# Elementwise work of two token mixers moved from GpSimd to VectorE in a two-layer hybrid diffusion block

## The chip, the cores and the metric

The kernel runs on one core of a Trainium2 chip. The metric is the time of one execution on the device in microseconds (us). Three runs of the kernel before took 3043.42, 3047.25 and 3040.82 us, median 3043.42. One more execution was taken under the hardware profiler; all rows of the profile below are of that one.

The engines are named as the profile names them: PE (TensorE, matmuls; PEld its weight loads), DVE (VectorE), ACT (ScalarE), POOL (GpSimd) and SP (SyncE, which here issues most DMAs). Each engine executes its own instructions strictly in the order in which the program gives them, and waits at an instruction until what it needs is there.

## The reference

Two layers over 1024 latent tokens and 256 context tokens of width 1024. In each layer one normalised input goes through one projection, whose columns are shared by three mixers that run side by side; their outputs are joined by one output projection, and a squared-ReLU MLP follows.

```python
h = modulate(rmsnorm(x, g_norm1[l]), sh1, sc1)
pf, mq, mk, mv, mo, mg, cq, ckv, kr = split_proj(h @ w_in[l])
y_f = fourier_mix(pf)                       # real part of a 2-D FFT over (positions, 64 channels)
hf, _ = mlstm_direction(fwd, st_f, False)   # forward and backward mLSTM, 4 heads of 96
hb, _ = mlstm_direction(bwd, st_b, True)
y_m = mlstm_output(hf, hb, mo, g_mlstm[l])  # rmsnorm(hf + hb) * g * sigmoid(mo)
y_a = merge_heads(blocked_attend(qn, qr, (lat_keys, ctx_keys)))   # 4 heads
x = x + ga1 * (jnp.concatenate([y_f, y_m, y_a], axis=-1) @ w_out[l])
x = x + ga2 * sqrelu_mlp(modulate(rmsnorm(x, g_norm2[l]), sh2, sc2), w_up[l], w_down[l])
```

The mLSTM is a recurrence over chunks with a state C per head, which the reference writes as

```python
h = num / jnp.maximum(jnp.abs(den), jnp.exp(-m_t))[..., None]
C_new = decay[..., None, None] * C + jnp.einsum("bhs,bhsd,bhsv->bhdv", wk, kb, vb)
```

where num and den hold the weights within a chunk, exp(dmat − m_t), and the state's part, weighted by w_inter. Everything is in fp32. In layer 0 the context tokens go through the same mixers; in layer 1 only the latent outputs are needed.

## The kernel before

Tokens are cut into ten chunks of 128 (eight latent, two context). Large matmuls run on two rounded halves of each fp32 operand: `split` (L145 to L148) writes the high part with a copy and the low part with a subtraction, and a product then takes three matmuls (L138, L143, L144). Intermediate results of the projection lie in HBM (du, dk, dq, dv for the mixers' inputs; dM and dW for the mLSTM's gate rows; dC for its states; dy for the outputs), and the mixers load them again in tiles.

Attention is the mixers' main work on PE. For each head and block of queries it runs over ten key tiles: three matmuls give the scores s, ACT takes their exponential PT (L1140), and a matmul adds PT times V to v (L1141); below, such a round is called an attention step. The row maxima are found ahead of time, by matmuls into m (L1003) and a reduction on DVE (L1004); a second reduction (L1010) joins them, PE transposes them (L1013), and a split puts them into a row of the queries Q. The queries of the next block are prepared by `q_piece` (rotary part at L989 to L991, then a split).

The other two mixers are written as generators, and `side_work()` pulls one step of them at a time between attention steps: first all of `mlstm`, then `fourier`. That fixes in which neighbourhood their instructions lie. The final order on each engine is set by a scheduler from its own model of the program, and is static: it can move an instruction ahead of others on its engine, but at run time every engine goes through its list in order.

`mlstm` has three parts.

- The recurrence (L825 to L853): 9 steps for each of two directions d, so 18 in a layer. A step loads a chunk's keys kc and values vc (`load_v`, with a memset of a column of ones), transposes the keys on PE (L834), copies them to kt, multiplies vc by a weight per row and head into wv (L839; the tile shares its buffers with Mb, and the profile calls it Mb), multiplies on PE (L842), and updates the state C on DVE (L850, four instructions; the tiles share their buffers with qw and Wb). C goes to dC.
- The output loop (L874 to L927): for each of 10 chunks (layer 1: 8) PE makes the scores sp (L885), and for both directions a step loads Mb and Wb, broadcast from rows of dM and dW; makes tm = mask − Mb (L897), its exponential on ACT (L900), its product with the scores (L901, DVE); qw = qc × Wb (L906), except in a direction's first chunk; and on PE the sums of tm times vc (L912) and qw times the state Cp (L914). DVE then makes the denominators dn (L918 to L920) and hd (L922).
- `tail` (L854 to L872), for the chunk before: hsum = both directions' hd (L856), its square on ACT, a reduction and `rstd_small` (L171 to L187), which is three rounds of L185, L186 and L187 on four columns; two products (L863, L865), three transposes on PE (L868), and the output's store.

`fourier` (L717 to L811) folds the columns of its input uT (the profile calls the tile krw) into sums `up` and differences `um` (L740, L741), folds those again on DVE (L751), and multiplies by tables on PE. It runs for two halves of the channels, in layer 0 for latent and context tokens.

The tiles Mb, tm, qw, Wb, vc and kc have two buffers each; ssb, up, um and uT have one.

Of the kernel before, what the change touches and what calls it, by code (L numbers as in the profile page):

```python
# [9 lines left out]
ALU = mybir.AluOpType  # L10
# [53 lines left out]
def build(tc, A, out, dbg=None):  # L64
# [41 lines left out]
    V, S, G, PE = nc.vector, nc.scalar, nc.gpsimd, nc.tensor  # L106
# [321 lines left out]
    for l in range(2):  # L428
# [83 lines left out]
        for b in range(3):  # L512
            t0, n, w = BLK[b]
            if b < 2 or ctx_all:
                for i in range(2):
# [3 lines left out]
                    o = T(wk, [128, 512], tag="ev")  # L519
# [128 lines left out]
        for n_, ti in enumerate((4, 5, 2, 3, 0, 1)):  # L648
# [18 lines left out]
            wv = cvh[:, ti * 5:ti * 5 + 5]  # L667
# [50 lines left out]
        def fourier(fo):  # L718
# [9 lines left out]
            for i in range(2):  # L728
# [5 lines left out]
                for (o, N, scl) in ((0, NL, 1.0), (NL, NCX, 2.0))[:2 if ctx_all else 1]:  # L734
                    lat = N == NL
                    H = N // 2
                    up = T(f0, [128, 513], tag="up")
                    um = T(f0, [128, 513], tag="um")
                    rev = uT[:, o + H:o + N][:, ::-1]
                    G.tensor_tensor(up[:, 1:H + 1], uT[:, o + 1:o + H + 1], rev, ALU.add)  # L740
                    G.tensor_tensor(um[:, 1:H], uT[:, o + 1:o + H], rev[:, :H - 1], ALU.subtract)  # L741
                    S.copy(up[:, 0:1], uT[:, o:o + 1])
                    S.copy(up[:, H:H + 1], uT[:, o + H:o + H + 1])
                    G.memset(um[:, 0:1], 0.0)
# [68 lines left out]
        def mlstm(mlp_):  # L813
# [12 lines left out]
            for p in range(9):  # L826
                for d in range(2):
                    ci = order[d][p]
                    kc = T(mlp_, [96, 4, 128], tag="kc", bufs=2)
                    nc.sync.dma_start(kc, dkh[:, :, tok(ci)])  # L830
                    vc = load_v(ci)
                    ps = T(psL, [128, 512], tag="l")
                    for h in range(4):
                        PE.transpose(ps[:, h * 96:(h + 1) * 96], kc[:, h, :], ident[:96, :96])  # L834
                    kt = T(mlp_, [128, 512], tag="tm", bufs=2)
                    S.copy(kt[:, :384], ps[:, :384])
                    wcol = wkT[:, 64 * d + ci:64 * d + ci + 31:10]
                    wv = T(mlp_, [128, 4, 128], tag="Mb", bufs=2)
                    G.tensor_tensor(wv[:, :, :97], vc, wcol.unsqueeze(2).to_broadcast([128, 4, 97]), ALU.mult)  # L839
                    pc = T(psL, [128, 512], tag="l")  # L840
                    for h in range(4):
                        PE.matmul(pc[:96, h * 97:(h + 1) * 97], kt[:, h * 96:(h + 1) * 96], wv[:, h, :97], start=True, stop=True)  # L842
                    C = T(mlp_, [96, 4, 128], tag=("qw", "Wb")[d], bufs=2)
                    pv = pc[:96, :388].rearrange("p (h e) -> p h e", h=4)
                    if p == 0:
                        S.copy(C[:, :, :97], pv)
                    else:
                        for h in range(4):
                            dcol = 40 * d + 10 * h + ci
                            V.scalar_tensor_tensor(C[:, h, :97], prev[d][:, h, :97], decb[:, dcol:dcol + 1], pv[:, h], ALU.mult, ALU.add)  # L850
                    prev[d] = C
                    nc.sync.dma_start(dC[d, ci].rearrange("p (h e) -> p h e", h=4), C[:, :, :97])
                    yield  # L853
            def tail(ci, hs, mo):  # L854
                hsum = hs[0]
                G.tensor_tensor(hsum, hs[0], hs[1], ALU.add)  # L856
                S.activation(hs[1], hsum, AF.Square)
                v4 = T(mlp_, [128, 4], tag="v4", bufs=2)
                V.tensor_reduce(v4, hs[1], AX.X, ALU.add)
                V.tensor_scalar(v4, v4, 1.0 / 96, EPS, ALU.mult, ALU.add)  # L860
                y4 = T(mlp_, [128, 4], tag="y4", bufs=2)
                rstd_small(y4, v4, 4, mlp_)
                V.tensor_tensor(hsum, hsum, y4.unsqueeze(2).to_broadcast([128, 4, 96]), ALU.mult)  # L863
                hf = hsum.rearrange("p h e -> p (h e)")
                V.scalar_tensor_tensor(mo, mo, 1.0, hf, ALU.add, ALU.mult)  # L865
                pt = T(psL, [128, 512], tag="l")
                for i in range(3):
                    PE.transpose(pt[:, i * 128:(i + 1) * 128], mo[:, i * 128:(i + 1) * 128], ident)  # L868
                ym = T(mlp_, [128, 3, 128], tag="ym", bufs=2)
                for i in range(3):  # L870
                    S.activation(ym[:, i], pt[:, i * 128:(i + 1) * 128], AF.Copy, scale=gmh[:, 3 * l + i:3 * l + i + 1])
                nc.sync.dma_start(dy[256:640].rearrange("(i p) t -> p i t", p=128)[:, :, tok(ci)], ym)  # L872

            pend = None  # L874
            for ci in range(10 if ctx_all else 8):
# [14 lines left out]
                for d in range(2):  # L890
# [3 lines left out]
                        v_ = src[64 * d:64 * d + 40].rearrange("(h c) t -> h c t", h=4)[:, ci, :]  # L894
                        nc.sync.dma_start(dst, v_.unsqueeze(0).to_broadcast([np_, 4, 128]))
                    tm = T(mlp_, [128, 4, 128], tag="tm", bufs=2)
                    G.tensor_tensor(tm, msk[:, d].unsqueeze(1).to_broadcast([128, 4, 128]), Mb, ALU.subtract)  # L897
                    for h in range(4):
                        col = 64 * d + 10 * h + ci
                        S.activation(tm[:, h], tm[:, h], AF.Exp, bias=aT[:, col:col + 1])  # L900
# [2 lines left out]
                    if not first:  # L903
                        pi = order[d][order[d].index(ci) - 1]
                        qw = T(mlp_, [96, 4, 128], tag="qw", bufs=2)
                        G.tensor_tensor(qw, qc, Wb, ALU.mult)  # L906
                        Cp = T(mlp_, [96, 4, 97], tag="Cp", bufs=2)
                        nc.sync.dma_start(Cp, dC[d, pi].rearrange("p (h e) -> p h e", h=4))
                    po = T(psL, [128, 512], tag="l")
# [792 lines left out]
```

## Time and profile before

| | us |
|---|---|
| runs | 3043.42, 3047.25, 3040.82 |
| median of the runs | 3043.42 |
| the profiled execution, its own time | 3047.78 |
| its span, first to last instruction | 3046.0 |
| mean granted TensorE clock in the span | 0.957 |
| mixers of layer 0 | 362 to 640 |
| recurrence; output loop; Fourier part of layer 0 | 362 to 430; 430 to 570; 570 to 640 |
| mixers of layer 1 | 1950 to 2200 |
| recurrence; output loop; Fourier part of layer 1 | 1950 to 2030; 2030 to 2150; 2150 to 2200 |

The stretches of the mixers were read from the first and last instruction of their lines; they overlap a little, as the scheduler mixes them, and the first loads of layer 1's Fourier part lie in its recurrence. How to read the rows: in a group, the columns are the line, the engine, the operation, what it writes and reads, shapes, the count (x), then busy us and mean ns, then idle time of the engine ahead of the group and who ended it. In a row in order of time the first two numbers are start and duration in us, and brackets hold the idle time ahead and its releaser. In a table of stretches, each engine's busy us (and count) stand in the order of the header line, then the granted clock, the share of the DMA engines and GB/s. A row of waits names the waiting engine, tile and line, the releaser, total us, times, and the longest.

### The profile page before, as it was taken

What the parts mean: (1) busy time and instruction counts of PE and PEld (TensorE: products, weight loads), DVE (VectorE), ACT (ScalarE), POOL (GpSimd) and SP (SyncE); (2) the same over time, 40 slices, a digit from 0 to 9 for tenths busy, and PEclk for the clock granted to TensorE, in tenths of its full rate; (3) what the DMA queues carried; (4) which work ended last, traced back from release to release, by engine and by line L of the source; (5) the groups of instructions that cost most, each with busy time, mean ns of one, the idle gap of its engine ahead of it and who ended that gap; (6) DMA issues with size and microseconds to landing.
All of it is one profiled execution on the core that took longest, in us unless ns stands there. A gap on an engine that the chain in (4) does not pass through costs nothing.

```text
span 3046.0 us, 40618 instructions
## 1 busy us (share of the span) xinstructions
PE 2841.8 (93%) x14320; PEld 2343.2 (77%) x14320; DVE 2112.7 (69%) x4034; ACT 1179.0 (39%) x2283; POOL 667.8 (22%) x653
## 2 busy tenths in 40 slices
PE   7998998998989999999999899898999899989996
PEld 6887875766868888788887788776767688868885
DVE  8769668642399899767787618368632976678887
ACT  3322244443353333333344523244432544434444
POOL 4212234111300000021224233233122000013334
PEclk7999999999989999999999999899999999999998
DMA  6514575223345544732131212365133443353321
GB/s 238 159 53 127 145 181 154 90 69 113 116 159 174 166 168 155 283 118 85 54 97 42 106 43 84 114 163 144 55 112 127 147 147 103 109 197 97 105 90 56
DMA packets 277872, 376.45 MB, mean 124 GB/s; under 512 B 63396, under 2 KB 154468, under 8 KB 276004
## 3 DMA queue, kind: packets, MB, share of 16 engines
q1 hardware_dynamic: 274788, 366.51, 38.5%
q0 software_dynamic: 576, 4.20, 0.4%
q10 hardware_dynamic: 2304, 3.15, 0.3%
q8 instruction: 113, 1.85, 0.3%
q14 instruction: 91, 0.75, 0.1%
HBM read 283.74 MB, written 90.02 MB: 123 GB/s over the span
## 4 chain that ended last, share of the span: by engine, by line
PE 57%; DVE 19%; DMA 10%; issue 6%; POOL 3%; ACT 3%; SPq 0%; DVEq 0%; POOLq 0%; ACTq 0%
PE mm L138 9%; PE mm L143 7%; PE mm L144 7%; PE v L1141 4%; PE mm L135 4%; PE mm L136 4%; PE mm L134 3%; DVE junk L235 3%; DMA wf<-in_w_mt 2%; DVE A L148 2%; DVE ac L677 2%; PE mm L1466 2%; PE mm L140 2%; PE mm L141 2%; DMA gt<-in_w_mt 2%
## 5 line engine op out<-in xcount | busy, mean ns | idle before, releaser
L138 PE MATMUL mm<-A,wr 128*128 128x512 f32 (+1 forms) x840 | 315.2, 378 | 23.5 <-ACT rb L673 9.7
L135 PE MATMUL mm<-A 128*128 128x512 f32 (+1 forms) x654 | 251.6, 390 | 12.0 <-DVE A L148 9.6
L134 PE MATMUL mm<-A 128*128 128x512 f32 (+1 forms) x654 | 238.2, 388 | 5.6 <-ACT A L147 4.5
L136 PE MATMUL mm<-A 128*128 128x512 f32 (+1 forms) x654 | 243.0, 387 | 0.3 <-DVE A L148 0.3
L138 PEld LDWEIGHTS mm<-A,wr 128*128 128x128 f32 x840 | 162.7, 195 | 53.7 <-ACT rb L673 11.4
L143 PE MATMUL mm<-A,wr 128*128 128x512 f32 (+1 forms) x520 | 196.2, 378 | 3.7 <-DVE A L148 1.6
L144 PE MATMUL mm<-A,wr 128*128 128x512 f32 (+1 forms) x520 | 193.7, 373 | 0.0
L1141 PE MATMUL v<-PT,Vt 128*97 128x512 f32 (+1 forms) x336 | 178.1, 616 | 12.9 <-ACT PT L1140 12.6
L138 PE MATMUL mm<-A,c 128*128 128x512 f32 (+1 forms) x520 | 184.4, 355 | 6.2 <-ACT A L147 5.0
L148 POOL TENSOR_TENSOR wr<-wf,wr 128x512 fp32r<-128x512 f32 x88 | 125.2, 1431 | 289.1 <-ACT wr L147 267.3
L143 PE MATMUL mm<-A,c 128*128 128x512 f32 (+1 forms) x520 | 184.8, 355 | 3.0 <-DVE A L148 2.9
L144 PE MATMUL mm<-A,c 128*128 128x512 f32 (+1 forms) x520 | 182.7, 353 | 1.2 <-DVE c L148 1.2
L147 ACT ACTIVATE A<-wr 128x512 fp32r<-128x512 f32 x188 | 114.2, 625 | 147.9 <-PE mm L135 59.2
L147 ACT ACTIVATE A<-A 128x512 fp32r<-128x512 f32 x174 | 107.0, 625 | 160.0 <-PE mm L135 86.5
L148 DVE TENSOR_TENSOR A<-wr,A 128x512 fp32r<-128x512 f32 x146 | 128.8, 894 | 43.3 <-ACT A L147 29.0
L135 PEld LDWEIGHTS mm<-A 128*128 128x128 f32 x654 | 123.9, 190 | 40.7 <-DVE A L148 12.9
L235 DVE SCALAR_TENSOR_TENSOR junk<-wf,t 128x512 bf16<-128x512 f32 x192 | 131.0, 682 | 32.8 <-DMA wf<-in_w_mt 31.1
L1140 ACT ACTIVATE PT<-s 128x512 f32<-128x512 f32 (+1 forms) x168 | 97.3, 583 | 134.1 <-PE s L144 133.7
L134 PEld LDWEIGHTS mm<-A 128*128 128x128 f32 x654 | 123.1, 189 | 31.2 <-ACT A L147 6.9
L136 PEld LDWEIGHTS mm<-A 128*128 128x128 f32 x654 | 123.5, 189 | 24.8 <-DVE A L148 0.7
L138 PE MATMUL mm<-wr,A 128*128 128x256 f32 x464 | 134.3, 290 | 6.6 <-ACT rb L673 4.7
L143 PE MATMUL mm<-wr,A 128*128 128x256 f32 x464 | 133.9, 289 | 0.0
(497 smaller groups left out, 7938.3 us busy)
## 6 DMA issues: line engine op xcount, KB each, us to landing
wf<-in_w_mt SPq DMA_DIRECT2D x96, 256.0 KB
x<-in_w_up SPq DMA_DIRECT2D x40, 512.0 KB
r<-in_w_up SPq DMA_DIRECT2D x38, 512.0 KB
wr<-in_w_dn SPq DMA_DIRECT2D x36, 512.0 KB
gt<-in_w_mt SPq DMA_DIRECT2D x64, 256.0 KB
da<-wf SPq DMA_DIRECT2D x64, 256.0 KB
da<-p SPq DMA_DIRECT2D x64, 256.0 KB
wf<-in_w_in SPq DMA_DIRECT2D x56, 256.0 KB
```

What stands on the lines that cost most here:

```text
L134: PE.matmul(ps, lh, rh, start=first, stop=False, skip_group_check=True)
L135: PE.matmul(ps, lh, rl, start=False, stop=False, skip_group_check=True)
L136: PE.matmul(ps, ll, rh, start=False, stop=last, skip_group_check=True)
L138: PE.matmul(ps, lh, rh, start=first, stop=False)
L140: PE.matmul(ps, ll, rh, start=False, stop=False)
L143: PE.matmul(ps, lh, rl, start=False, stop=False)
L144: PE.matmul(ps, ll, rh, start=False, stop=last)
L147: (hi or S).activation(dst[0], src, AF.Copy) if (hi is None or hi is S) else hi.tensor_copy(dst[0], src)
L148: (lo or G).tensor_tensor(dst[1], src, f32(dst[0]), ALU.subtract)
L235: V.scalar_tensor_tensor(junk, f, 1.0, cb[w], ALU.mult, ALU.mult, accum_out=(ga, modT[l])[kh][:, w, j:j + 1])
L1140: S.activation(PT[:, :nq], ps[:, :nq], AF.Exp, scale=scale)
L1141: PE.matmul(po[:97, :nq], Vt[kt // 2][:, kt % 2, h % 2], PT[:, :nq], start=i == 0, stop=i == len(kts) - 1)
```

## The change

Six elementwise instructions are written for VectorE (`V.`) where they were written for GpSimd (`G.`). Operands, shapes and everything else stay. In a whole run that is 136 instructions: 36 of L839, 18 of L856, 36 of L897, 34 of L906, and 6 each of L740 and L741. GpSimd keeps in these stages the memsets (vc's ones, um's ends) and splits of attention's operands.

```diff
@@ fourier
                     rev = uT[:, o + H:o + N][:, ::-1]
-                    G.tensor_tensor(up[:, 1:H + 1], uT[:, o + 1:o + H + 1], rev, ALU.add)
-                    G.tensor_tensor(um[:, 1:H], uT[:, o + 1:o + H], rev[:, :H - 1], ALU.subtract)
+                    V.tensor_tensor(up[:, 1:H + 1], uT[:, o + 1:o + H + 1], rev, ALU.add)
+                    V.tensor_tensor(um[:, 1:H], uT[:, o + 1:o + H], rev[:, :H - 1], ALU.subtract)
@@ mlstm, recurrence
                     wv = T(mlp_, [128, 4, 128], tag="Mb", bufs=2)
-                    G.tensor_tensor(wv[:, :, :97], vc, wcol.unsqueeze(2).to_broadcast([128, 4, 97]), ALU.mult)
+                    V.tensor_tensor(wv[:, :, :97], vc, wcol.unsqueeze(2).to_broadcast([128, 4, 97]), ALU.mult)
@@ mlstm, tail
                 hsum = hs[0]
-                G.tensor_tensor(hsum, hs[0], hs[1], ALU.add)
+                V.tensor_tensor(hsum, hs[0], hs[1], ALU.add)
@@ mlstm, output loop
                     tm = T(mlp_, [128, 4, 128], tag="tm", bufs=2)
-                    G.tensor_tensor(tm, msk[:, d].unsqueeze(1).to_broadcast([128, 4, 128]), Mb, ALU.subtract)
+                    V.tensor_tensor(tm, msk[:, d].unsqueeze(1).to_broadcast([128, 4, 128]), Mb, ALU.subtract)
...
                         qw = T(mlp_, [96, 4, 128], tag="qw", bufs=2)
-                        G.tensor_tensor(qw, qc, Wb, ALU.mult)
+                        V.tensor_tensor(qw, qc, Wb, ALU.mult)
```

What the change does to the order on an engine is shown at three places, as the difference of the two programs' lists (− stands only in before at this place, + only in after; a name is a tile with a running number; x is a count).

On DVE in layer 0's output loop, inside a tail (y, rs_t, hd and mo are the tail's; tm, qw and dn belong to the output step of a later chunk):

```order
 L187 SCALAR_TENSOR_TENSOR y_861_4466<-rs_t_4470,y_861_4466 128x4
 L863 TENSOR_TENSOR hd_786_4198<-hd_786_4198,y_861_4466 128x384
+L865 SCALAR_TENSOR_TENSOR mo_4153<-mo_4153,hd_786_4198 128x384
+L901 TENSOR_TENSOR tm_4379<-tm_4379,ssb_4363 128x512
+L901 TENSOR_TENSOR tm_4422<-tm_4422,ssb_4363 128x512
+L897 TENSOR_TENSOR tm_4537<-msk_3489,Mb_4533 128x512
 L918 SCALAR_TENSOR_TENSOR dn_4399<-l_4390,flT_1253 128x4
-L865 SCALAR_TENSOR_TENSOR mo_4153<-mo_4153,hd_786_4198 128x384
+L906 TENSOR_TENSOR qw_4544<-qc_4506,Wb_4534 96x512
 L919 TENSOR_TENSOR dn_4399<-l_4390,dn_4399 128x4
```

The moved L897 and L906 now stand among the tail's and the denominators' short instructions, and the tail's last product (L865) ahead of two L901 and one L897.

On DVE at the start of layer 1's recurrence (Mb here is wv of L839; the tiles of L850 called qw and Wb are states; um and fd belong to the Fourier part, Q and mx to attention):

```order
+L839 TENSOR_TENSOR Mb_16856<-vc_16846,wkT_14941 128x4x97
 L991 TENSOR_TENSOR qf_16908<-qf_16908,q_2718_16910 32x512
-L751 TENSOR_TENSOR fd_19155<-um_19145 128x256 x2
+L850 SCALAR_TENSOR_TENSOR qw_16832<-qw_16751,decb_14943,l_16827 96x97 x4
+L741 TENSOR_TENSOR um_19326<-krw_19312 128x511
 L148 TENSOR_TENSOR Q_16900<-qf_16908,Q_16900 96x512
-L850 SCALAR_TENSOR_TENSOR qw_16832<-qw_16751,decb_14943,l_16827 96x97 x4
+L850 SCALAR_TENSOR_TENSOR Wb_16863<-Wb_16804,decb_14943,l_16858 96x97 x4
 L1004 TENSOR_REDUCE mx_16941<-m_16942 128x1
+L839 TENSOR_TENSOR Mb_16887<-vc_16877,wkT_14941 128x4x97
```

Each L839, which needs a load of vc, is now in the list of the state updates and of attention's reductions, and L741, which needs the load of krw, is in front of a split of Q.

On PE in layer 0's output loop, around the transposes of the first tail (L868; the rows L138 to L144 and L1141 are attention steps, m is of the row maxima):

```order
-L868 MATMUL l_4327<-cst_60,mo_4053 128x128 x3
-L885 MATMUL l_4358<-qc_4351,kc_4349 128x128 x4
+L1013 MATMUL m_5054<-cst_60,m_1022_5052 1x128 x4
 L1141 MATMUL v_4688<-PT_4977,Vt_591_3484 97x512
 L138 MATMUL s_5016<-Q_4286,x_586_3479 128x512
 L143 MATMUL s_5016<-Q_4286,x_586_3479 128x512
 L144 MATMUL s_5016<-Q_4286,x_586_3479 128x512
+L1141 MATMUL v_4688<-PT_5020,Vt_592_3485 97x512
+L138 MATMUL s_5045<-Q_4286,x_586_3479 128x512
+L143 MATMUL s_5045<-Q_4286,x_586_3479 128x512
+L144 MATMUL s_5045<-Q_4286,x_586_3479 128x512
+L868 MATMUL l_4327<-cst_60,mo_4053 128x128 x3
```

The transposes now stand behind two L1141 and two rounds of scores that came after them before. Over a layer, ahead of the last tail's transposes stand 48 matmuls of L1141's kind where 43 stood in layer 0, and 137 where 131 stood in layer 1.

## The prediction

> **What bounds the kernel now.** I read the share of each engine first, then the stretches in which the moved lines run, engine by engine, then PE's waits in them.
> ```profile
> PE 2841.8 (93%) x14320; PEld 2343.2 (77%) x14320; DVE 2112.7 (69%) x4034; ACT 1179.0 (39%) x2283; POOL 667.8 (22%) x653
> ```
> Over the whole run PE is the bound. The moved lines run only where the mixers do, 362 to 640 and 1950 to 2200 us, so the question is what PE lacks there. The stretches are layer 0's recurrence and output loop, then layer 1's:
> ```profile
> core 0: us, PE busy (x) PEld busy (x) DVE busy (x) ACT busy (x) POOL busy (x), PEclk, DMA share, GB/s
> 362.00:430.00 68.00, 61.69 (x414) 49.37 (x412) 41.03 (x115) 26.18 (x55) 20.53 (x45) 0.95 0.79 179
> 430.00:570.00 140.00, 116.27 (x637) 87.75 (x636) 113.92 (x277) 65.98 (x171) 58.55 (x55) 0.91 0.54 144
> 1950.00:2030.00 80.00, 67.42 (x435) 54.94 (x434) 47.06 (x117) 28.48 (x58) 26.67 (x52) 0.89 0.71 172
> 2030.00:2150.00 120.00, 109.84 (x583) 83.06 (x582) 95.16 (x230) 58.24 (x145) 47.69 (x45) 0.91 0.50 133
> ```
> PE is idle 6.3 + 23.7 + 12.6 + 10.2 = **52.8 us** in these 408 us, and its clock is below full: no gain can be larger than that idle time and what of the clock comes back with it. In the output loops DVE is 81% and 79% full, so it has little room for more work, on its face. The next rows are why its fullness is not what it seems: layer 0's output loop, DVE and POOL in order of time.
> ```profile
> 454.75 1.31 POOL L897 TENSOR_TENSOR tm<-msk,Mb 128x512 f32<-128x512 f32 x1 [0.88 <-ACT PT L1140]
> ...
> 454.94 1.13 DVE L185 TENSOR_TENSOR rs_t<-y 128x4 f32<-128x4 f32 x1
> ...
> 456.06 1.28 POOL L906 TENSOR_TENSOR qw<-qc,Wb 96x512 f32<-96x512 f32 x1
> ...
> 456.11 1.25 DVE L186 TENSOR_TENSOR rs_t<-rs_t,rs_h 128x4 f32<-128x4 f32 x1
> 457.39 0.16 DVE L187 SCALAR_TENSOR_TENSOR y<-rs_t,y 128x4 f32<-128x4 f32 x1
> ...
> 457.59 0.16 DVE L185 TENSOR_TENSOR rs_t<-y 128x4 f32<-128x4 f32 x1
> ```
> A DVE instruction on four columns takes 1.13 and 1.25 us, and ends when the GpSimd instruction beside it ends; the same line takes 0.16 us 1.4 us after. So a two-operand instruction of DVE waits, within its duration, for GpSimd's to finish. The busy time of DVE in these stages holds GpSimd's time a second time.
>
> **The change part by part.** All six lines become DVE instructions. What they cost on GpSimd, over the run:
> ```profile
> L897 POOL TENSOR_TENSOR tm<-msk,Mb 128x512 f32<-128x512 f32 x36 | 46.8, 1299 | 117.8 <-PE l L912 83.6 <-DVE qf L991 10.8 <-PE m L144 9.1
> L906 POOL TENSOR_TENSOR qw<-qc,Wb 96x512 f32<-96x512 f32 x34 | 45.5, 1337 | 8.7 <-DMA Wb<-dW 4.4 <-DVE q L990 3.7 <-PE l L914 0.5
> L839 POOL TENSOR_TENSOR Mb<-vc,wkT 128x388 f32<-128x388 f32 x36 | 31.3, 873 | 65.8 <-PE l L842 37.0 <-DMA vc<-dv 24.1 <-PE m L1003 4.8
> L856 POOL TENSOR_TENSOR hd<-hd,hd 128x384 f32<-128x384 f32 x18 | 18.2, 1013 | 55.0 <-DVE hd L922 55.0
> L740 POOL TENSOR_TENSOR up<-krw 128x512 f32<-128x512 f32 (+1 forms) x6 | 6.0, 997 | 36.9 <-PE l L769 36.7
> L741 POOL TENSOR_TENSOR um<-krw 128x511 f32<-128x511 f32 (+1 forms) x6 | 6.0, 996 | 22.9 <-PE l L763 15.6 <-ACT fd L753 4.7 <-DMA krw<-du 2.6
> ```
> That is 153.8 us. On DVE the nearest rows are two-operand instructions of the same shapes (minimum, median and maximum in ns):
> ```profile
> L901 DVE TENSOR_TENSOR tm<-tm,ssb x36: 673/685/1452, 433.1 to 2147.2; 128x512 f32<-128x512 f32 x36
> L865 DVE SCALAR_TENSOR_TENSOR mo<-mo,hd x18: 542/558/1523, 460.9 to 2163.2; 128x384 f32<-128x384 f32 x18
> L186 DVE TENSOR_TENSOR rs_t<-rs_t,rs_h x111: 139/161/2433, 73.1 to 3038.0; 128x4 f32<-128x4 f32 x90, 128x2 f32<-128x2 f32 x21
> L991 DVE TENSOR_TENSOR qf<-qf,q x16: 682/683/2864, 368.1 to 2226.3; 32x512 f32<-32x512 f32 x16
> ```
> **Added to DVE:** 70 instructions of L897 and L906 at 0.685 = 48.0 us, 54 of L839 and L856 at 0.558 = 30.1 us, and 12 of L740 and L741, of which eight are of 512 elements and four of 128, at most 0.685 each = under 8; I take 6.5. Sum 84.6 us. The Trainium skill, "GPSIMD Engine Reference", section 3.1 on elementwise work, puts GpSimd at 1.96 times DVE for such an instruction; by that page the estimate would be 78.5 us, and the rows' 1299 against 685 (1.90) agree.
>
> **Taken from DVE:** the waits inside its instructions. Layer 0's output loop, then layer 1's, at count, sum and mean:
> ```profile
> L186 DVE TENSOR_TENSOR rs_t<-rs_t,rs_h 128x4 f32<-128x4 f32 x24 | 12.0, 498 | 0.6
> L187 DVE SCALAR_TENSOR_TENSOR y<-rs_t,y 128x4 f32<-128x4 f32 x24 | 11.4, 476 | 0.4
> L185 DVE TENSOR_TENSOR rs_t<-y 128x4 f32<-128x4 f32 x24 | 8.7, 364 | 0.5
> L863 DVE TENSOR_TENSOR hd<-hd,y 128x384 f32<-128x384 f32 x8 | 7.5, 940 | 0.4
> L865 DVE SCALAR_TENSOR_TENSOR mo<-mo,hd 128x384 f32<-128x384 f32 x8 | 6.1, 758 | 0.1
> L991 DVE TENSOR_TENSOR qf<-qf,q 32x512 f32<-32x512 f32 x3 | 3.9, 1305 | 0.1
> ```
> ```profile
> L185 DVE TENSOR_TENSOR rs_t<-y 128x4 f32<-128x4 f32 x20 | 8.3, 417 | 0.4
> L186 DVE TENSOR_TENSOR rs_t<-rs_t,rs_h 128x4 f32<-128x4 f32 x20 | 7.4, 371 | 0.4
> L187 DVE SCALAR_TENSOR_TENSOR y<-rs_t,y 128x4 f32<-128x4 f32 x20 | 7.4, 369 | 0.4
> L865 DVE SCALAR_TENSOR_TENSOR mo<-mo,hd 128x384 f32<-128x384 f32 x6 | 5.2, 863 | 0.1
> ```
> With 0.161 for the small, 0.558 for the 384-wide and 0.683 for L991, layer 0 gets back 8.1 + 7.6 + 4.9 + 3.1 + 1.6 + 1.9 = 27.2 us, layer 1 5.1 + 4.2 + 4.2 + 1.8 = 15.3. Added in the same stretches: layer 0 38 instructions at 0.685 and 9 at 0.558 = 31.0; layer 1 32 and 7 = 25.8. So DVE goes from 113.9 to **117.7 of 140** and from 95.2 to **105.7 of 120**: about as full as before, with GpSimd's 106 us of these stretches off the board. In the recurrences 18 instructions add 10 us each to 41 of 68 and 47 of 80: room enough, but for order (below).
>
> **What of it is on PE's path.** PE's waits that hang on GpSimd or on DVE's stretched chain, layer 0 and then layer 1 (total, times, longest):
> ```profile
> PE l L868 <- DVE dn L918: 10.6, 5, 2.8
> ...
> PE m L1013 <- DVE m L1010: 2.9, 1, 2.9
> PE m L1003 <- DVE mx L1004: 2.3, 2, 2.1
> ```
> ```profile
> PE l L842 <- POOL Mb L839: 9.6, 5, 5.5
> PE l L868 <- DVE dn L919: 6.2, 3, 3.8
> PE l L914 <- POOL qw L906: 2.5, 1, 2.5
> ```
> L868 are the transposes that end a tail, the chain of some fifteen short DVE instructions of which the stretched L185 to L187 (three rounds of each) are the middle. Of these 34.1 us I leave 5.5 in place: the longest L839 wait also needs its load of vc, which lands just ahead of it. 28.6 remain. From below they can all stay, since DVE is as full as before (that they grow is the second rival); from above they can all go. I take **half, 14.3**: a tail's instructions no longer pay 1.2 us each, but share their queue with 0.685 us ones. The third order piece above points the same way: two more rounds of attention's scores and L1141 fill PE ahead of the transposes. In the two output loops and layer 1's recurrence the clock's shortfall is 0.09 × 140 + 0.09 × 120 + 0.11 × 80 = 32 us-equivalents; if it follows the idle time, of which 14.3 of 46.5 go, that is 10; I take half, **5**.
>
> **What it costs.** GpSimd waited for loads with nothing of weight behind it; DVE's queue has. The rows above give vc 24.1, Wb 4.4 and krw 2.6 us; Mb is
> ```profile
> POOL tm L897 <- DMA Mb<-dM: 7.1, 1, 7.1
> ```
> In all 38.2 us. Most were waits of an engine that ran ahead, and DVE arrives later. In layer 1's recurrence L839 now stands ahead of L850 (the state that releases PSUM) and L1004 (softmax scores for PE's L1013), so a late vc holds both: **3 us** of the 24.1, between 0 and 24.1. There too um stands ahead of the split of Q, so a late krw delays PE's attention: **2 us**, between 0 and 2.6. In layer 0 and layer 1 the first L897 stands ahead of L850; PE was idle around it before, so 0, up to 7.1. Wb costs 0, up to 4.4: DVE reaches it behind L897, whose load was issued first. L856 opens the tail, and is part of the half taken for L868. L740 and L741 release the Fourier part's folds (L751), and in its stretch of layer 0 PE lacks 1.2 us of 70:
> ```profile
> 570.00:640.00 70.00, 68.80 (x375) 50.26 (x373) 36.97 (x104) 28.25 (x70) 5.55 (x10) 1.00 0.19 62
> ```
> So they gain nothing there, and cannot cost much either, with DVE half full. GpSimd keeps the memsets of these stages and its splits, which now start no later than before; I count nothing for them.
>
> **Sum:** −14.3 − 5 + 3 + 2 = −14.3 us. The profiled execution took 3047.8 us (span 3046.0 and 1.8 around it), so 3033.5; it is 4.4 above the median of 3043.4, so 3029.1, which I give as 3030. A change under 0.2% (6.1 us) can't be told from none here.
>
> **The rivals.** *Even exchange, about 3043.* DVE is as full after as before, and the tail still waits its turn. For it: 117.7 of 140 against 113.9. Against: the POOL waits of PE (12.1 us) end sooner whatever DVE does, since 0.685 replaces 1.3. The Trainium skill, "Perfetto Trace Analysis", section on optimizing Scalar/DVE operations, says that because the two engines share an SBUF read port, moving work between them may not help; the stretched rows above show the sharing, but in them GpSimd's instruction takes twice as long as DVE's would, which that sentence leaves out. Its outcome would be this rival's time.
>
> *Head of the line, slower, about 3055.* DVE takes its queue in order. Where a load of vc, Mb, Wb or krw lands after DVE gets there, everything behind it stands: L1004, L850, the splits of Q. It decides the sign from the point where DVE arrives at such a line ahead of its load by more, summed over a layer's 18 recurrence steps, than the 7 us (half of 14.3) that a layer gains; GpSimd's 38.2 us of such waits are its ceiling, and a third to a half of it, 12 to 19 us, less a small gain of 4, gives 3051 to 3058. For it: DMA is 79% and 71% busy in the recurrences. Against: 24.1 of the 38.2, those for vc, come from instructions that GpSimd reached with nothing else to do, while DVE in the recurrences has 41 of 68 and 47 of 80 us of older work in front of them, which uses up part of each wait.
>
> *The whole of it, about 3012.* All 28.6 go, and the clock pays 5: 33.6 less a little cost, 3012. For it: in PE's new order 48 attention steps (one L1141 each in that list) lie ahead of layer 0's last tail where 43 did, and 137 where 131 did in layer 1, so that PE has more to do while a tail runs. Against: DVE's fullness, and that a tail is a chain, whose links wait for what stands between them in the queue.
>
> That the change doesn't do what it says is out: all 136 instructions stand in DVE's order and none in GpSimd's.
>
> **How the numbers follow.** Forecast (3018 to 3037) 0.40, even exchange (3037 to 3049) 0.25, head of the line 0.18, the whole 0.17. Faster: the forecast and the whole, 0.57; same 0.25; slower 0.18. Low 3010 takes in the whole; high 3056 most of the slower rival.
>
> **What would show it.** Right: L185 to L187 near 0.16 us throughout, PE's waits at L868 halved, DVE near 118 and 106 in the same stages, both stages shorter by 5 to 10 us. Even exchange: L868's waits unchanged with L185 short. Head of the line: DVE idle before L839, L897 or L906 on a DMA, and PE's waits for L1010 or L148 grown. The prediction is wrong at its root if L897 on DVE takes over 1 us, or if L185 stays near 0.4 without GpSimd beside it.

## The result, and the profile after

The changed kernel took 3016.85 us (median of four runs, 3013.96 to 3020.10) where the kernel before took 3042.12 (four runs, 3038.17 to 3047.25): a ratio of **0.9915**, 95% interval 0.9899 to 0.9932, so 25.3 us faster. A second comparison on another occasion gave 0.9909 (0.9896 to 0.9921). The forecast was 3030 in a range of 3010 to 3056, that is 13.4 us faster than the 3043.4 known then: the direction and the range held, but the gain was nearly twice the forecast one. The profiled execution after took 3019.14 us with a span of 3017.3, 28.6 us less than the profiled one before.

Where the time went is seen from stretches with fixed ends: from a layer's first transposed key (L834) to its last attention matmul (L1141), in which each kernel does the same work. Before, then after, layer 0 and layer 1:

```profile
core 0: us, PE busy (x) PEld busy (x) DVE busy (x) ACT busy (x) POOL busy (x), PEclk, DMA share, GB/s
365.80:745.60 379.80, 337.66 (x1766) 247.48 (x1767) 227.63 (x559) 157.48 (x362) 100.54 (x117) 0.95 0.46 122
1960.20:2276.50 316.30, 290.58 (x1497) 215.75 (x1498) 200.63 (x468) 134.84 (x294) 90.02 (x102) 0.93 0.47 127
```
```profile
363.90:722.90 359.00, 330.41 (x1767) 244.53 (x1767) 232.24 (x627) 156.53 (x361) 21.88 (x44) 0.96 0.48 129
1935.70:2247.90 312.20, 290.29 (x1498) 216.70 (x1498) 210.21 (x530) 135.33 (x294) 20.74 (x40) 0.93 0.48 128
```

Layer 0 became 20.8 us shorter and layer 1 4.1. Length less PE's busy time is PE's idle time: 42.1 and 25.7 us before, 28.6 and 21.9 after, so 13.5 and 3.8 us of idle time went. PE's matmuls are the same in the trace but for one record in each layer; they took 7.3 us less in layer 0 (a better clock, 0.96 for 0.95) and 0.3 less in layer 1. DVE, which took some 79 us of GpSimd's work in layer 0, is busy only 4.6 us more there. A second profiled execution of the changed kernel (e6) has 352.9 and 311.7 for the two layers, so in layer 0 differences of less than about 6 us between single profiles are not read below; in layer 1 the two profiles agree to 0.5 us.

DVE's groups in the two output loops, in the windows of the prediction (layer 0's, then layer 1's):

```profile
L897 DVE TENSOR_TENSOR tm<-msk,Mb 128x512 f32<-128x512 f32 x19 | 13.0, 686 | 3.7 <-PE l L912 3.4 <-DMA Mb<-dM 0.2
L906 DVE TENSOR_TENSOR qw<-qc,Wb 96x512 f32<-96x512 f32 x18 | 12.2, 679 | 3.9 <-DMA Wb<-dW 3.9
L185 DVE TENSOR_TENSOR rs_t<-y 128x4 f32<-128x4 f32 x28 | 4.4, 157 | 0.5
L186 DVE TENSOR_TENSOR rs_t<-rs_t,rs_h 128x4 f32<-128x4 f32 x27 | 4.2, 157 | 0.5
L187 DVE SCALAR_TENSOR_TENSOR y<-rs_t,y 128x4 f32<-128x4 f32 x27 | 4.2, 156 | 0.5
```
```profile
L186 DVE TENSOR_TENSOR rs_t<-rs_t,rs_h 128x4 f32<-128x4 f32 x24 | 3.8, 160 | 0.5
```

The small instructions have their 0.16 us everywhere, where their means were 0.36 to 0.50 us before, and tm and qw take 0.686 and 0.679 instead of 1.3. PE's waits in layer 0's mixers and in layer 1's, the lines that answer to those of before:

```profile
PE m L1003 <- DVE mx L1004: 0.4, 1, 0.4
...
PE l L868 <- DVE dn L920: 0.2, 1, 0.2
```
```profile
PE l L842 <- DVE Mb L839: 7.2, 2, 5.2
PE m L1003 <- DVE mx L1004: 3.8, 4, 1.6
PE m L1013 <- DVE m L1010: 3.5, 3, 1.9
...
PE l L868 <- DVE hd L922: 0.4, 1, 0.4
```

The waits at the tails' transposes went almost altogether: 10.6 to 0.2 and 6.2 to 0.4 us. In layer 1 the wait at L1003 is new (0.3 us before, over the whole layer); that at L1013 is not, as the layer had 3.1 us of it before, late in its stretch.

### The profile page after: what moved, and what is told of

Its sections match the earlier page's. It is cut to its first block, busy times and chain, and to the rows that moved or that the text cites. A ratio compares the mean times of both kernels' runs of the same rounds, so it can differ in the third digit from the quotient of the medians.

```text
span 3017.3 us, 40556 instructions
## 1 busy us (share of the span) xinstructions
PE 2827.9 (94%) x14320; PEld 2334.7 (77%) x14320; DVE 2128.6 (71%) x4170; ACT 1178.6 (39%) x2283; POOL 517.3 (17%) x517
## 4 chain that ended last, share of the span: by engine, by line
PE 59%; DVE 18%; DMA 10%; issue 6%; POOL 2%; ACT 2%; SPq 0%; DVEq 0%; POOLq 0%; ACTq 0%
PE mm L138 9%; PE mm L143 7%; PE mm L144 7%; PE v L1141 4%; PE mm L135 4%; PE mm L136 4%; PE mm L134 4%; DVE junk L235 3%; DVE A L148 2%; DVE ac L677 2%; PE mm L1466 2%; PE mm L140 2%; PE mm L141 2%; DMA wf<-in_w_mt 2%; PE t L1466 2%
## 5 line engine op out<-in xcount | busy, mean ns | idle before, releaser
L138 PE MATMUL mm<-A,wr 128*128 128x512 f32 (+1 forms) x840 | 312.9, 375 | 24.6 <-ACT rb L673 12.3
L138 PEld LDWEIGHTS mm<-A,wr 128*128 128x128 f32 x840 | 161.2, 193 | 54.0 <-ACT rb L673 14.0
L143 PE MATMUL mm<-A,wr 128*128 128x512 f32 (+1 forms) x520 | 193.0, 372 | 6.2 <-DVE A L148 4.2
L144 PE MATMUL mm<-A,wr 128*128 128x512 f32 (+1 forms) x520 | 191.6, 369 | 0.0
L1141 PE MATMUL v<-PT,Vt 128*97 128x512 f32 (+1 forms) x336 | 172.8, 599 | 16.6 <-ACT PT L1140 16.1
L138 PE MATMUL mm<-A,c 128*128 128x512 f32 (+1 forms) x520 | 184.0, 355 | 4.5 <-ACT A L147 3.4
L144 PE MATMUL mm<-A,c 128*128 128x512 f32 (+1 forms) x520 | 182.5, 353 | 1.3 <-DVE c L148 1.3
L148 POOL TENSOR_TENSOR wr<-wf,wr 128x512 fp32r<-128x512 f32 x88 | 123.7, 1413 | 292.1 <-ACT wr L147 230.3
L148 DVE TENSOR_TENSOR A<-wr,A 128x512 fp32r<-128x512 f32 x146 | 128.7, 893 | 43.4 <-ACT A L147 29.0
L138 PE MATMUL mm<-wr,A 128*128 128x256 f32 x464 | 133.4, 288 | 6.6 <-ACT rb L673 4.7
```

The source lines that it names most:

```text
L138: PE.matmul(ps, lh, rh, start=first, stop=False)
L143: PE.matmul(ps, lh, rl, start=False, stop=False)
L144: PE.matmul(ps, ll, rh, start=False, stop=last)
L148: (lo or G).tensor_tensor(dst[1], src, f32(dst[0]), ALU.subtract)
L1141: PE.matmul(po[:97, :nq], Vt[kt // 2][:, kt % 2, h % 2], PT[:, :nq], start=i == 0, stop=i == len(kts) - 1)
```

## The experiments

Four theories were set against each other. **A**: the shared port; GpSimd's instructions stretch DVE's, and that lateness reaches PE (in a narrow form at the transposes L868, in a wide form through how full DVE is). **B**: own durations; each moved line is shorter on PE's path by its own 0.6 us. **C**: the scheduler's new order alone. **D**, formed after e4: the stretch costs because the order was planned without it. (No run looks into the scheduler's model; that it leaves the stretch out is what D assumes.)

All ratios are to the kernel before, run beside the experiment on the same chip; the numbers of attention steps are counted in PE's list, as in the order pieces above. Those of layer 1, above and in the expectations, are counted from the program's start and hold the 88 steps of layer 0: 131 and 137 are 43 and 49 of layer 1's own 80. Below they are given within the layer. The expectations name the experiments' theories by these letters.

**e1: tm and qw alone,** on the kernel before, as are e2, e5, e8, e9, e10 and e12.
```diff
-                    G.tensor_tensor(tm, msk[:, d].unsqueeze(1).to_broadcast([128, 4, 128]), Mb, ALU.subtract)
+                    V.tensor_tensor(tm, msk[:, d].unsqueeze(1).to_broadcast([128, 4, 128]), Mb, ALU.subtract)
...
-                        G.tensor_tensor(qw, qc, Wb, ALU.mult)
+                        V.tensor_tensor(qw, qc, Wb, ALU.mult)
```


> Only L897 and L906 (tm, qw) go to VectorE; L839, L856, L740 and L741 stay on GpSimd. Theory A (shared port): the gain comes from the tail's short DVE instructions no longer being stretched by a GpSimd instruction beside them, and tm and qw are what runs beside the tails: 18 to 23 us faster than before (about 3020 to 3024), L186 in layer 0's output loop near 0.2 us, PE's waits at L868 below 3 us in each layer. Theory B (own durations): each moved instruction saves its own 0.6 us on PE's path, so the gain goes with the moved GpSimd time, 92.3 of 153.8 us: about 15 us faster, with L842's waits of layer 1 unchanged. Theory C (order alone): PE's list has L868 behind nearly the same attention steps as in the changed kernel (48 and 138), so all of the gain, 25 us.

Measured 0.9906 (0.9886 to 0.9925), 28 us faster: all of the gain, with 60% of the moved GpSimd time. Theory B, which priced by each line's own time, expected 15, and theory A 18 to 23; the 25 of theory C are nearest.

**e2: wv of the recurrence alone.**
```diff
-                    G.tensor_tensor(wv[:, :, :97], vc, wcol.unsqueeze(2).to_broadcast([128, 4, 97]), ALU.mult)
+                    V.tensor_tensor(wv[:, :, :97], vc, wcol.unsqueeze(2).to_broadcast([128, 4, 97]), ALU.mult)
```


> Only L839 (wv of the recurrence) goes to VectorE. Theory A: the tails keep their GpSimd neighbours, so 0 to 4 us faster, out of L842's waits in layer 1 alone (9.6 us before). Theory B: 31.3 of 153.8 us of GpSimd time, so about 5 us. Theory C: in layer 1 L868 stands as late as in the changed kernel (136 attention steps ahead of the last tail against 137), in layer 0 45 against 48: 8 us or more.

Measured 1.0017 (1.0002 to 1.0032): no gain, if anything a loss. Theory C falls in its plain form, as L868 stands nearly as late in layer 1's list as in the changed kernel (48 steps against 49), and layer 1's mixers took 316.5 us, as before (316.3).

**e4: the changed kernel with GpSimd loaded again.**
```diff
-            pend = None
+            pend = None; dum = T(mlp_, [128, 4, 128], tag="dum")
...
                     V.tensor_tensor(tm, msk[:, d].unsqueeze(1).to_broadcast([128, 4, 128]), Mb, ALU.subtract)
+                    G.tensor_tensor(dum, msk[:, d].unsqueeze(1).to_broadcast([128, 4, 128]), Mb, ALU.subtract)
...
                         V.tensor_tensor(qw, qc, Wb, ALU.mult)
+                        G.tensor_tensor(dum[:96], qc, Wb, ALU.mult)
```


> The changed kernel, and beside each L897 and L906 of VectorE the same instruction once more on GpSimd, into a tile that nothing reads. PE's list stands nearly as in the changed kernel. Theory A: the stretch of L185 to L187 returns (means of 0.35 to 0.5 us instead of 0.16 in layer 0's output loop), PE waits at L868 again by over 8 us in layer 0, and 12 to 25 us of the 25 gained are lost: 3029 to 3042. Also the moved instructions themselves get stretched. Theory B and theory C: nothing waits for the added instructions and the order is that of the changed kernel: 3014 to 3021.

Measured 1.0019 (1.0007 to 1.0031): the whole gain is lost to instructions whose result nobody reads. Its layers, and DVE's groups in layer 0's output loop:

```profile
359.20:731.80 372.60, 336.20 (x1766) 248.76 (x1767) 254.55 (x627) 156.94 (x361) 75.39 (x82) 0.94 0.46 124
1940.00:2267.30 327.30, 299.05 (x1498) 221.55 (x1498) 225.87 (x531) 135.25 (x294) 65.30 (x72) 0.91 0.45 123
```
```profile
L897 DVE TENSOR_TENSOR tm<-msk,Mb 128x512 f32<-128x512 f32 x20 | 16.3, 816 | 8.6 <-PE l L912 4.7 <-DMA Mb<-dM 3.8
L906 DVE TENSOR_TENSOR qw<-qc,Wb 96x512 f32<-96x512 f32 x18 | 14.7, 816 | 2.1 <-DMA Wb<-dW 2.1
L922 DVE TENSOR_TENSOR hd<-l,dn 128x384 f32<-128x384 f32 x20 | 10.9, 551 | 0.2
L185 DVE TENSOR_TENSOR rs_t<-y 128x4 f32<-128x4 f32 x30 | 8.1, 271 | 0.5
L186 DVE TENSOR_TENSOR rs_t<-rs_t,rs_h 128x4 f32<-128x4 f32 x30 | 6.0, 198 | 0.5
```

DVE does the same 627 instructions of layer 0 as in the changed kernel, and is busy 254.6 us instead of 232.2: the stretch is GpSimd's doing. It falls on two-operand instructions in SBUF, tm and qw too (0.816 for 0.686 and 0.679), and not on all of DVE: L922, whose wide operand is in PSUM, has 0.551 us here and 0.552 in the changed kernel. But the tail's small instructions are stretched less than expected (0.20 to 0.27 us), and PE's waits at L868 stayed below 3 us in layer 0: the loss does not sit at the transposes. One thing is mixed in: PE waited 3.0 us at L912 for GpSimd's added instructions, and the one result of GpSimd that L912 uses is the memset of vc, which stands behind them. That is 3.0 of the 7.8 us by which PE's idle time in layer 0 grew (28.6 to 36.4), so e4 does not show the price of the stretch by itself.

**e5: the port as before, the transposes later.**
The second half of tail, from its transposes on, becomes a function of its own, which is called one chunk later:
```diff
+            def tail2(ci, mo):
                 pt = T(psL, [128, 512], tag="l")
...
-                        tail(*pend)
+                        tail(*pend); pend2 = (pend2 and tail2(*pend2), (pend[0], pend[2]))[1]
...
-                mo = T(mlp_, [128, 384], tag="mo", bufs=2)
+                mo = T(mlp_, [128, 384], tag="mo", bufs=3)
```


> The kernel before, all six lines on GpSimd, but the transposes that end a tail (L868) and what follows them are written one chunk later, with a third buffer for mo. The port stays as contended as before. Theory A in its narrow form (PE's waits at L868 are where the stretch costs): these waits go (16.8 us over both layers), and with the clock 12 to 20 us are gained: 3022 to 3030. Theory A in a wide form (DVE's fullness sets the pace of the whole output loop) and theory B: PE finds other waits instead, below 5 us gained: 3037 to 3045. Theory C predicts a gain only where L868 stands later among the attention steps than before, which here is so in layer 1 (135 against 131) and not in layer 0 (42 against 43): about 4 us.

Measured 1.0014 (0.9999 to 1.0029). PE's waits at L868 fell from 10.6 to 7.0 us in layer 0 and from 6.2 to 1.5 in layer 1, and nothing was gained: at L885 PE waited 3.4 and 4.5 us instead of 1.2 and 0.7, and the last tail's transposes stand no later in layer 0's list (42 steps). This speaks against the narrow form of theory A, by which L868 is where the lateness costs; but half of the 16.8 us was still there, so it is not a clean test.

**e6: the changed kernel again.**

> The changed kernel once more, so that the next three stand beside it on the same chip: 0.9915 of before, within 0.9899 to 0.9932.

Measured 0.9909 (0.9896 to 0.9921).

**e7: the same DVE load, on DVE's own account.**
The two added lines of e4, on the other engine:
```diff
-                    G.tensor_tensor(dum, msk[:, d].unsqueeze(1).to_broadcast([128, 4, 128]), Mb, ALU.subtract)
+                    V.tensor_tensor(dum, msk[:, d].unsqueeze(1).to_broadcast([128, 4, 128]), Mb, ALU.subtract)
...
-                        G.tensor_tensor(dum[:96], qc, Wb, ALU.mult)
+                        V.tensor_tensor(dum[:96], qc, Wb, ALU.mult)
```


> The changed kernel with each L897 and L906 done twice on VectorE, the second time into a tile that nothing reads: some 26 us more of DVE work in layer 0's output loop and 22 in layer 1's, which is what the added GpSimd instructions cost DVE before (27.9 and 16), but on DVE's own account, known to the scheduler, and without a port held by another engine. Theory A, wide form (how full DVE is sets the pace, however it comes to be full): all or nearly all of the gain is lost, 0.997 to 1.004 of before. Theory D (what costs is that the stretch falls on instructions whose place was planned without it): the scheduler puts L868 behind 64 attention steps in layer 0 instead of 48, PE is fed, and at least half of the gain stays, 0.991 to 0.996.

Measured 0.9990 (0.9980 to 1.0000). By the total theory A had it, but the layers tell two things apart:

```profile
360.70:717.40 356.70, 331.09 (x1762) 245.72 (x1762) 254.51 (x664) 156.33 (x360) 20.41 (x43) 0.95 0.47 129
1929.20:2261.10 331.90, 299.24 (x1496) 221.81 (x1497) 230.18 (x563) 135.89 (x294) 20.70 (x40) 0.91 0.45 121
```

In layer 0 DVE is as busy as in e4 (254.5 and 254.6 us), and the layer takes 356.7 us instead of 372.6, as short as in the changed kernel. There, DVE work that the order was planned with costs nothing that can be told, and as much of it made by GpSimd's added instructions costs 16 us, with the wait for the memset in it and with another list (64 steps in e7, 53 in e4). In layer 1 both cost about the same (331.9 and 327.3 against 312.2): there the list put hardly more attention ahead of the last tail (52 steps against 49), and why it did not is open.

**e8: hsum alone.**
```diff
-                G.tensor_tensor(hsum, hs[0], hs[1], ALU.add)
+                V.tensor_tensor(hsum, hs[0], hs[1], ALU.add)
```


> Only L856, the sum that opens a tail, goes to VectorE. Theory A: 18 instructions of 1.0 us go from the port, of 92 + 18 us beside the output loops, and DVE gets 10 us more: within 0.2% of before, 0.998 to 1.001. The rival (the tail's chain sets PE's waits, link by link): each tail is 0.45 us shorter by L856 itself, 18 tails, 8 us: 0.996 to 0.998.

Measured 0.9976 (0.9963 to 0.9989): 7 us, as the rival had it. Here the order changed too (46 attention steps ahead of the last tail of layer 0 instead of 43), so the run does not show which of the two it was.

**e9: tm, qw and hsum, without the recurrence's and the Fourier part's lines.** The edit is that of e1 and e8 together.

> L897, L906 and L856 on VectorE, L839, L740 and L741 left on GpSimd. If the lines of the recurrence and of the Fourier part only fill DVE's queue (L839 alone gave 1.0017), this is 0.1 to 0.3% faster than the changed kernel: 0.988 to 0.991. If they pay for themselves where the others are moved too: 0.991 to 0.994.

Measured 0.9908 (0.9896 to 0.9921), against 0.9909 of the changed kernel beside it. So in the whole time L839, L740 and L741 bring nothing and cost nothing that can be told, where the others are moved. The profiles of layer 1 say otherwise: it took 302.8 us in e1 and 304.1 in e9, which leave these lines on GpSimd, and 312.2 and 311.7 in the two of the changed kernel (308.0 in e13). Outside the two stretches e9 took 2348.1 us and e6 2342.0, which makes the totals equal; why is open.

**e10: the kernel before, with one pacing number changed.**
```diff
-RM = (0.5, 0.8)
+RM = (0.9, 0.8)
```


> The kernel before with one number changed: the share of attention's steps over which layer 0's mLSTM is spread, 0.9 instead of 0.5. GpSimd and the port stay as they were. In PE's list of layer 0 the last tail's transposes then stand behind 47 attention steps instead of 43 (48 in the changed kernel), in layer 1 behind 136 instead of 131. Theory D (in layer 0 the stretch costs because the order was planned without it, and PE has other work to put there): layer 0's mixers 8 to 15 us shorter, 0.995 to 0.997 of before in all. Theory A alone (DVE as full, port as contended): 0.999 to 1.002. Theory C (order alone explains the change): 0.991.

Measured **0.9939** (0.9925 to 0.9954), about 19 us faster: more than theory D expected (0.995 to 0.997) and less than theory C (0.991). GpSimd still does all six lines:

```profile
361.80:720.00 358.20, 330.49 (x1766) 245.15 (x1767) 220.87 (x559) 156.23 (x362) 101.10 (x117) 0.96 0.47 129
1928.30:2243.10 314.80, 288.72 (x1496) 212.67 (x1497) 195.33 (x468) 135.07 (x294) 91.05 (x102) 0.93 0.47 128
```

Layer 0 is as short as in the changed kernel (358.2 against 359.0), with GpSimd at 101.1 us as before; layer 1 is as long as before (314.8 against 316.3), though its list has moved to 48 steps. PE's waits at L868 in layer 0 are 3.2 us. The stretch is not quite that of before, however: over layer 0, before and then e10,

```profile
L186 DVE TENSOR_TENSOR rs_t<-rs_t,rs_h 128x4 f32<-128x4 f32 x30 | 12.9, 430 | 0.8
L187 DVE SCALAR_TENSOR_TENSOR y<-rs_t,y 128x4 f32<-128x4 f32 x30 | 12.4, 412 | 0.5
L185 DVE TENSOR_TENSOR rs_t<-y 128x4 f32<-128x4 f32 x30 | 9.7, 323 | 0.7
```
```profile
L187 DVE SCALAR_TENSOR_TENSOR y<-rs_t,y 128x4 f32<-128x4 f32 x30 | 9.5, 317 | 0.6
L186 DVE TENSOR_TENSOR rs_t<-rs_t,rs_h 128x4 f32<-128x4 f32 x30 | 9.1, 303 | 0.7
L185 DVE TENSOR_TENSOR rs_t<-y 128x4 f32<-128x4 f32 x30 | 7.9, 264 | 0.7
```

These three lines took 35.0 us before and 26.5 in e10, where in the changed kernel they take 14.1, so some two fifths of their stretch went with the new list and the rest stayed. DVE's busy time in layer 0 fell by 6.8 us for the same 559 instructions.

**e11 and e12: L922 to ACT,** in the changed kernel and in the kernel before.
```diff
-                    V.tensor_tensor(hd, pv[:, :, 0:96], dn.unsqueeze(2).to_broadcast([128, 4, 96]), ALU.mult)
+                    for h in range(4): S.activation(hd[:, h], pv[:, h, 0:96], AF.Copy, scale=dn[:, h:h + 1])
```


> The changed kernel with L922 (hd from PSUM times 1/dn, 0.55 us on DVE, 36 of them) done by ACT in four pieces: 20 us less DVE work over both layers (about 11 and 9), 20 to 35 us more on ACT, which was half full in the output loops. Theory A (in layer 1 DVE's fullness sets the pace): layer 1's mixers 4 to 9 us shorter than in the changed kernel, layer 0's 0 to 4: 0.987 to 0.990 of before. If DVE's work is no longer what sets the pace once GpSimd is gone: as the changed kernel, 0.990 to 0.993; if ACT's exponentials (L900, L1140) wait behind it, slower than that.

> The kernel before, GpSimd's six lines in place, with L922 on ACT. DVE is relieved of the same 20 us, with the port as contended as before. Theory A: fullness counts however it is made, so 20 of the 41 us (of the stretch) that the change took away come off here too: 0.994 to 0.997. Theory D and the narrow form (the stretch itself, inside the tail's chain): 0.998 to 1.001.

Measured 0.9898 (0.9881 to 0.9914) for e11, not to be told from the changed kernel, and 1.0026 (1.0011 to 1.0041) for e12. In e12 DVE was busy 214.9 us in layer 0's mixers instead of 227.6, and they took 381.6 us instead of 379.8. A less busy DVE alone gains nothing, though ACT was 16.4 us busier for it (173.9 for 157.5), an addition that in e11 (17.3 us) left layer 0 as it was. In layer 1 too, e12 and e11 took 315.5 and 311.2 us, where the kernels without this edit took 316.3 and 312.2. So the wide form of theory A has no support in these two runs.

**e13: the changed kernel, paced slower.** The edit is `RM = (0.82, 0.8)`.

> The changed kernel with layer 0's mLSTM spread over 0.82 of attention's steps. In PE's list of layer 0 the last tail's transposes stand behind 53 attention steps instead of 48. Theory D: PE's waits of layer 0 that are left (26 us of idle time, of which under 3 us at L868, L912 and L914) are not of this kind, so 0 to 3 us: 0.989 to 0.992 of before. If PE's list still lacks filler: 0.986 to 0.989.

Measured 0.9890 (0.9873 to 0.9907), the lowest of all, but its interval meets that of the changed kernel.

Layer 0 in all these kernels, in the order of the attention steps that stand ahead of its last tail's transposes (length and DVE busy time in us, from the profiles):

| kernel | steps | length | DVE busy |
|---|---|---|---|
| e5 | 42 | 375.0 | 226.8 |
| before | 43 | 379.8 | 227.6 |
| e12 | 44 | 381.6 | 214.9 |
| e2 | 45 | 382.5 | 230.3 |
| e8 | 46 | 368.7 | 230.7 |
| e10 | 47 | 358.2 | 220.9 |
| changed (two profiles) | 48 | 359.0, 352.9 | 232.2, 232.2 |
| e1; e9 | 48 | 357.1; 353.1 | 220.2; 224.3 |
| e11 | 52 | 358.3 | 224.4 |
| e13 | 53 | 351.5 | 233.4 |
| e4 (GpSimd loaded besides) | 53 | 372.6 | 254.6 |
| e7 | 64 | 356.7 | 254.5 |

Length does not go with DVE's busy time; with the steps it does: 375 us and more up to 45 steps, 359.0 and less from 47 on, except in e4, where GpSimd's load is added. The number of steps is only one mark of a whole order. A reading that fits all rows is theory D's, that PE is fed in layer 0 when the list puts enough attention ahead of mLSTM steps at the pace that these really have; the runs don't prove it. For layer 1 the steps tell nothing: 48 in e10 with 314.8 us, 49 in e9 with 304.1 and in the changed kernel with 312.2.

## Why the prediction was right, point by point

**The stretch** of DVE's small instructions by GpSimd was read rightly: 0.16 us throughout after, and back again in e4. **DVE's fullness** was forecast at 117.7 of 140 and 105.7 of 120 us; in the same windows it is

```profile
430.00:570.00 140.00, 130.57 (x752) 98.74 (x751) 120.39 (x362) 71.61 (x183) 1.38 (x9) 0.98 0.55 149
2030.00:2150.00 120.00, 115.44 (x616) 88.71 (x617) 101.80 (x298) 58.92 (x140) 1.09 (x6) 0.94 0.50 130
```

120.4 and 101.8, though the second window holds a later part of layer 1 than before. The Trainium skill, "Perfetto Trace Analysis", in its section on optimizing Scalar/DVE operations, doubts that moving work between these two engines helps because they share a port; in layer 0 here DVE took some 79 us of GpSimd's work for 4.6 us of its own busy time, and the kernel was 25.3 us faster.

**The terms of the sum.** The profiled pair differs by 28.6 us: 24.9 in the two stretches and 3.7 outside them. PE's idle time holds the path's gain and the costs together: forecast −14.3 + 5 = −9.3 us, measured −17.3 (13.5 + 3.8). The clock term was −5; PE's busy time fell by 7.6 (7.3 + 0.3). So the sum was short by 8.0 and 2.6 us in the stretches. The mis-sized step is "**half**": half of 28.6 us of waits was held back because DVE would be as full as before. Of these waits about 26 us went, those at L868 almost whole (16.8 to 0.6 us); other waits came in their place, so that the idle time fell by 17.3. In layer 0, e7 and e12 speak against fullness as a brake: there a DVE load that the list is planned with costs nothing that can be told, and relief alone gains nothing. The costs of 5 us (vc 3, krw 2) are not settled: the whole time of e9 beside e6 shows none (0.9908 against 0.9909), the profiles of layer 1 differ by 8 to 9 us between e9 or e1 and the changed kernel.

**The place.** "Both stages shorter by 5 to 10 us" was wrong: layer 0 gained 20.8 us and layer 1 4.1. In layer 1 the wait left in place (L842, 5.5 us) did stay, at 5.2, and a new wait of 3.8 us for the row maxima came (L1003). It is not in e1 and e9, where L839, L740 and L741 stay on GpSimd.

**The reason.** The prediction named the stretch as the cause, and the larger order in PE's list only as support for its "whole of it" rival. e10 turns this about for layer 0: a new list, with all of GpSimd's work and most of the stretch in place, makes the layer as short as the change does, and brings 0.9939 where the change brings 0.9915. e4 points the other way: with a list that has even more steps ahead, and GpSimd loaded again, the gain is gone, though part of that loss is the wait for the memset. Both fit if what counts is the match of list and pace; that is argued, not shown. How much of the 21 us in layer 0 comes from the new list and how much from the missing stretch is not settled, since no kernel here has the changed kernel's list with exactly the stretch of before. That the time fell inside the range is therefore in part luck: the sum priced the stretch's waits, and a new list, which the prediction took for a side effect, brings as much in layer 0 with GpSimd's work left where it was.

**The rivals.** *Even exchange* is out. *Head of the line*: the waits came, as DVE stood for loads of vc, Mb and Wb:

```profile
L897 DVE TENSOR_TENSOR tm<-msk,Mb 128x512 f32<-128x512 f32 x36 | 24.7, 686 | 14.4 <-DMA Mb<-dM 9.8 <-PE l L912 4.3
L906 DVE TENSOR_TENSOR qw<-qc,Wb 96x512 f32<-96x512 f32 x34 | 23.1, 679 | 7.5 <-DMA Wb<-dW 7.5
L839 DVE TENSOR_TENSOR Mb<-vc,wkT 128x388 f32<-128x388 f32 x36 | 20.0, 561 | 19.5 <-DMA vc<-dv 6.0 <-PE l L842 5.3 <-issue 4.4
```

These loads made DVE wait 23.3 us in all, against GpSimd's 35.6 for the same three, and those of krw 4.5 against 2.6. A small part of it reached PE, at the place that the prediction named. In layer 1's recurrence L741 stood for krw, the split of Q (L148), the state update and L1004 stood behind it, and PE's L1003 waited:

```profile
1951.95 0.69 DVE L741 TENSOR_TENSOR um<-krw 128x511 f32<-128x511 f32 x1 [1.48 <-DMA krw<-du]
...
1952.56 0.68 DVE L148 TENSOR_TENSOR Q<-qf,Q 96x512 fp32r<-96x512 f32 x1
1953.16 0.98 DVE L850 SCALAR_TENSOR_TENSOR Wb<-Wb,decb,l 96x97 f32<-96x97 f32 x4
...
1954.06 0.68 DVE L1004 TENSOR_REDUCE mx<-m 128x1 f32<-128x512 f32 x1
...
1954.80 0.79 PE L1003 MATMUL m<-x,Q 96*128 96x512 f32 x1 [1.57 <-DVE mx L1004]
```

Alone, wv on DVE did not pay (e2, 1.0017). So this rival is out as the sign of the change, not as a cost. *The whole of it*, about 3012, was nearest: 3016.85 lies below the band of 3018 to 3037 that the forecast itself was given.

## What to carry to other kernels

Where GpSimd and VectorE work side by side on SBUF, read the busy time of VectorE's two-operand instructions against their shortest durations: what lay above them here was GpSimd's time, and moving 79 us of GpSimd's work over cost VectorE 4.6 us in layer 0. Then ask whether a static list keeps the pace that the engines really have, and try the pacing number before moving any work: here one constant gave about 19 us of the 25. Don't brake an estimate by an engine's fullness alone; ask whether the engine that waits has other work to put in that place.

## What was not expected of the hardware

Both engines lose by the stretch, but not alike. In e4 the added GpSimd copies took means of 1.328 us (L897) and 1.474 (L906), where the same instructions took 1.299 and 1.337 in the kernel before; DVE's L897 and L906 beside them had 0.816 instead of 0.686 and 0.679, and its busy time in layer 0 rose by 22.3 us for the same 627 instructions. And less idle time came with a faster PE: in layer 0, 13.5 us less idle time with 7.3 us less busy time for the same matmuls in the changed kernel, and 14.4 with 7.2 in e10.
